# Matmul and transfer durations of a list schedule set to recorded ones

## The chip, the cores and the metric

The kernel runs on one core of one Trainium2 chip. A core has a matrix engine (TensorE, PE in the profile, with its weight loads as PEld), VectorE (DVE), ScalarE (ACT), GpSimd (POOL) and SyncE (SP), which here issues all DMA transfers between the chip's memory and the core's SBUF. TensorE writes its results to PSUM, which has eight banks of 512 words per partition. The metric is the time of one execution in microseconds on the device; lower is better.

## The reference

One layer of a decoder for 512 tokens of width 1024, in float32. A conditioning vector gives shift, scale and gate of two sub-layers (1024 x 6144 weights, `w_ada`). The mixer has two branches, joined by gates and an output projection; then comes an MLP with a squared ReLU.

```python
mod = c_act @ w_ada[l] + b_ada[l]
shift1, scale1, gate1, shift2, scale2, gate2 = [...]
h = rms_norm(x, g_pre_mix[l]) * (1.0 + scale1) + shift1
y = token_mixer(h, ...)
x = x + gate1 * rms_norm(y, g_post_mix[l])
h = rms_norm(x, g_pre_mlp[l]) * (1.0 + scale2) + shift2
y = jnp.square(jax.nn.relu(h @ w_mlp_in[l])) @ w_mlp_out[l]
x = x + gate2 * rms_norm(y, g_post_mlp[l])

# token_mixer
z = h @ w_in                               # 1024 x 4800
u = ua * jax.nn.sigmoid(ub)
u = causal_depthwise_conv(u, conv_w, conv_b)         # 31 taps
y_a = jax.nn.silu(layer_norm(u, ...)) @ w_conv_out
o = mla_attention(q_nope, q_rope, k_nope, k_rope, v) # 8 heads, causal
y_b = o @ w_attn_out
return (g_a * y_a + g_b * y_b) @ w_out
```

## The kernel before

**Arithmetic.** Most products are done on pairs: an operand is split into a high part (rounded to the engine's fp32r type by an ACT copy) and a low part (the difference, by a DVE subtraction), and a product is three matmuls, high x high, high x low, low x high (`mm3`). So each weight tile goes through a DMA load into the float arena (`f_arena`), an ACT cast and a DVE subtraction into the rounded arena (`r_arena`), and only then to TensorE (`wunit`, `W`).

**Stages, in program order.** The opening loads x, the parts of `w_ada` for the first modulation and the first columns of `w_in`, and multiplies them as they come. Then come the rest of `w_in` (gated-linear-unit columns, latents), attention head by head, the 31-tap convolution on DVE spread out between them (`pump`), `w_attn_out`, the two gates, the convolution branch's normalisation, `w_conv_out`, and `w_out`. The other parts of `w_ada` are accumulated on DVE (`ada_units`, one 1 MB load and two 128x1024 multiply-adds per step) at places set by `take`; parts 2 to 4 lie around the gates, `w_conv_out` and the beginning of `w_out`. After the norm between the sub-layers comes the MLP in four chunks; its second product uses Strassen's scheme with seven block products per chunk. The two arenas take 22400 and 28000 words per partition.

**The order of the work.** No instruction is issued when the program names it. `Planner.record` notes each one as an `Op` with its dependencies and a cost from `Planner.cost`: `o.cost`, the time for which it holds its engine, and `o.post`, the delay until its result can be used. `Planner.plan` then simulates the five engines:

- a first pass adds up TensorE's costs in program order; each TensorE op's sum is its deadline (`o.dead`), and the deadline of every other op is worked back from the ops that use it, with `o.cost`, `o.post` and, for a transfer, its bytes over 180 per ns;
- then, at each moment, every free engine takes from its heap of ready ops the one with the smallest key: on TensorE the program rank (`o.rank`, less a boost in a few places), on DVE, ACT, POOL and SP the deadline less `o.hurry`;
- a transfer holds SP for `o.cost`, starts 1100 ns after its issue or when the one modelled DMA path is free, takes its bytes over a rate, and lands 910 ns later.

`Planner.issue` (L383) emits the ops in that order, so each engine's instruction order is fixed by the plan, and on the chip each engine waits for semaphores where the plan's times don't hold.

**The places of buffers.** `Arena.alloc` and `Banks.alloc` give each buffer its place in SBUF or PSUM. A first emission has no times; after each plan, `Planner.lives` gives for every buffer the time from which it's wanted and the time at which it's let go, and the next emission places the buffers by these (`past`). A load's wanted time is at the earliest its deadline less `LEAD` (15000 ns). `emit` is repeated up to `PASSES` (8) times, and the plan with the smallest `plan.length` (the latest modelled end) is issued, its places replayed. So a duration in `cost` acts in three ways: on the order, on the places, and on which of the plans is taken.

All instructions that a plan issues have the profile's line L388, where they are emitted.

Of the kernel before, what the change touches and what calls it, by code (L numbers as in the profile page):

```python
# [53 lines left out]
class Arena:  # L54
# [11 lines left out]
    def __init__(self, tensor, words, past=None, replay=None):  # L66
        self.t = tensor
        self.n = words // self.G
        self.freed = [0.0] * self.n
        self.owner = [None] * self.n  # L70
        self.gone = []
        self.places = []
        self.past, self.replay = past, replay
        self.clock = 0.0
# [86 lines left out]


class Op:
    __slots__ = ("i", "eng", "fn", "a", "k", "cost", "post", "deps", "succ", "dead", "t0", "t1", "ndep", "ready", "dma", "rank", "hurry", "bufs", "raw")


class Planner:
# [6 lines left out]
    def __init__(self, nc, spaces):  # L174
        self.spaces = spaces
        self.real = dict(pe=nc.tensor, act=nc.scalar, dve=nc.vector, pool=nc.gpsimd, sp=nc.sync)
        self.ops = []
        self.last_w = {}
        self.reads = {}
        self.boost = 0  # L180
        self.hurry = 0.0
        self.after = None

    class Engine:
        def __init__(self, plan, name):
            self.plan, self.name = plan, name
# [30 lines left out]
    def cost(self, eng, fn, outs, ins, k):  # L217

        n = max(self.free_size(o) for o in (ins if fn == "reduce_sum" else outs))
        if fn == "dma_start":  # L220
            return 475.0, 2000.0
        psum = any(r.tensor.name.startswith("psum") for r in ins + outs)
        if eng == "pe":
            if fn == "transpose":
                return 0.85 * n + 1, 190.0
            if ins[0].dtype == F32:
                return max(53.5, n / 2.4 + 2) * 4, 190.0
            return max(64.0, n / 2.4 + 2.5), 190.0
        scalars = sum(isinstance(v, bass.AP) and self.free_size(v) == 1 for v in ins) if n > 1 else 0
        if eng == "act":  # L230
            t = 0.833 * n + (51 if psum else 93) + 93 * scalars
            if fn == "activation" and any(isinstance(v, bass.AP) for v in outs[1:]):
                t += 93
            return t, 150.0
        if eng == "dve":
            if fn in ("tensor_copy", "tensor_scalar"):
                return (1.04 if psum else 0.52) * n + 68 + 61 * scalars, 150.0
            if fn == "scalar_tensor_tensor":
                return 1.04 * n + 130, 150.0
            return 1.04 * n + 70, 150.0  # L240
        if fn == "memset":
            return 36.0, 100.0
        return (460.0 if ALU.pow in self.args else 160.0) + 1.0 * n, 150.0

    def record(self, eng, fn, a, k):
        self.args = a
        aps = [v for v in a if isinstance(v, bass.AP)]
        names = dict(k)
        outs, ins = [], []
        if "out" in names:  # L250
            outs.append(names.pop("out"))
        else:
            outs.append(aps.pop(0))
        if fn == "tensor_tensor_reduce":
            outs.append(aps.pop())
        if isinstance(names.get("accum_out"), bass.AP):
            outs.append(names.pop("accum_out"))
        ins = aps + [v for v in names.values() if isinstance(v, bass.AP)]
        o = Op()
        o.i, o.eng, o.fn, o.a, o.k = len(self.ops), eng, fn, a, k  # L260
        o.succ, o.dma, o.rank, o.hurry = [], None, len(self.ops) - self.boost, self.hurry
        o.cost, o.post = self.cost(eng, fn, outs, ins, k)
        if fn == "dma_start":
            b = 4
            for _, c in outs[0].ap:
                b *= c
            o.dma = b
        deps = set()
        rd = [self.region(r) for r in ins]
        wr = [self.region(w) for w in outs]  # L270
        o.bufs = set()
        for nm, units in rd + wr:
            for sp in self.spaces:
                if nm.startswith(sp):
                    o.bufs.add((sp, self.spaces[sp].owner[units[0]]))
        for nm, units in rd:
            lw, rs = self.last_w.setdefault(nm, {}), self.reads.setdefault(nm, {})
            for u in units:
                if u in lw:
                    deps.add(lw[u])  # L280
        o.raw = set(deps)
        for nm, units in wr:
            lw, rs = self.last_w.setdefault(nm, {}), self.reads.setdefault(nm, {})
            for u in units:
                if u in lw:
                    deps.add(lw[u])
                if u in rs:
                    deps.update(rs[u])
        for nm, units in rd:
            rs = self.reads[nm]  # L290
            for u in units:
                rs.setdefault(u, []).append(o.i)
        for nm, units in wr:
            lw, rs = self.last_w[nm], self.reads[nm]
            for u in units:
                lw[u] = o.i
                rs.pop(u, None)
        deps.discard(o.i)
        if self.after is not None:
            deps.add(self.after)  # L300
        o.deps = deps
        for d in deps:
            self.ops[d].succ.append(o.i)
        self.ops.append(o)

    def plan(self):
        ops = self.ops
        pe_t = 0.0
        big = sum(o.cost for o in ops if o.eng == "pe") + TAIL
        for o in ops:  # L310
            o.dead = big
            if o.eng == "pe":
                pe_t += o.cost
                o.dead = pe_t
        for o in reversed(ops):
            lat = o.post + (o.dma / 180.0 if o.dma else 0.0)
            for s in o.succ:
                q = ops[s]
                o.dead = min(o.dead, q.dead - q.cost - lat)
        heaps = {e: [] for e in self.NAMES}  # L320
        free = {e: 0.0 for e in self.NAMES}
        dma_free = 0.0
        future = []

        def key(o):
            return (o.rank, o.i) if o.eng == "pe" else (o.dead - o.hurry, o.i)

        for o in ops:
            o.ndep, o.ready = len(o.deps), 0.0
            if not o.ndep:  # L330
                heapq.heappush(future, (0.0, o.i))
        order = []
        now = 0.0
        while len(order) < len(ops):
            while future and future[0][0] <= now:
                o = ops[heapq.heappop(future)[1]]
                heapq.heappush(heaps[o.eng], (key(o), o.i))
            for e in self.NAMES:
                if free[e] <= now and heaps[e]:
                    o = ops[heapq.heappop(heaps[e])[1]]  # L340
                    o.t0 = now
                    free[e] = now + o.cost
                    if o.dma:
                        st = max(now + 1100.0, dma_free)
                        dma_free = st + o.dma / 360.0
                        o.t1 = dma_free + 910.0
                    else:
                        o.t1 = free[e] + o.post
                    order.append(o)
                    for s in o.succ:  # L350
                        q = ops[s]
                        q.ndep -= 1
                        q.ready = max(q.ready, o.t1 if (q.eng != o.eng or o.dma) else free[e] if e == "pe" else max(free[e], o.t1 - 30))
                        if not q.ndep:
                            heapq.heappush(future, (q.ready, q.i))
            nxt = [free[e] for e in self.NAMES if free[e] > now and heaps[e]]
            if future:
                nxt.append(future[0][0])
            if not nxt:
                break  # L360
            now = max(now, min(nxt)) if min(nxt) > now else now
        assert len(order) == len(ops)
        self.length = max(o.t1 for o in ops)
        return order
# [1270 lines left out]
```

## Time and profile before

| | |
|---|---|
| time, median of 3 runs | 832.8 us (831.78 to 833.91) |
| time of the profiled execution | 832.68 us |
| its span, first to last instruction | 830.9 us |
| mean granted TensorE clock | 0.994 |
| ACT busy in the span | 422.4 us (51%) |
| DMA, all queues | 117.28 MB, mean 141 GB/s |

The page splits the span into 40 slices of 20.8 us. A digit is a slice's busy share in tenths; PEclk is the granted clock and DMA the busy share of the 16 DMA engines.

```profile
PE   6989999999999999999999989999999999999995
DVE  4979989999999999998999589298529993975696
PEclk9999999999999999999999999999999999999998
DMA  9998423201464140062799362065014831660302
```

A group of instructions is shown with its engine, its operation, output and inputs with their shapes, its count, its busy time, the mean duration of one, and the engine's idle time just ahead with what ended it. Instructions overlap in an engine's pipeline, so a busy time is less than count times mean. A row of busy times by stretch has the stretch in us from the span's start, its length, and then for PE, PEld, DVE, ACT and POOL the busy time with the count, then the granted clock, the DMA share and GB/s. A timeline row has start, duration, engine, line, operation and count.

### The profile page before, as it was taken

Reading aid. Unit: us, or ns where it says so; the run is one execution under the profiler, and the core shown is the slowest. Engines: PE = TensorE matmul, PEld = TensorE weight load, DVE = VectorE, ACT = ScalarE, POOL = GpSimd, SP = SyncE. Lnnn points to the kernel's source line nnn. Section 1 sums busy time; section 2 is a strip of 40 time slices with the busy share of each in tenths; the row PEclk is TensorE's granted clock in tenths of the full one; section 3 lists DMA queues with packets and bytes.
Section 4 is the critical chain, followed back from the end, with each engine's and each line's share of the span. In section 5 each row is a group of like instructions: output and inputs, shape, how many; then the busy total and the mean of one; then the engine's idle time right before and its main releaser. Section 6 shows DMA issues by size and latency. Waiting matters only on the chain.

```text
span 830.9 us, 10647 instructions
## 1 busy us (share of the span) xinstructions
PE 805.1 (97%) x3940; PEld 672.5 (81%) x3940; DVE 686.6 (83%) x1012; ACT 422.4 (51%) x712; POOL 26.4 (3%) x84
## 2 busy tenths in 40 slices
PE   6989999999999999999999989999999999999995
PEld 3867888889987888888877879888888888888884
DVE  4979989999999999998999589298529993975696
ACT  5364273275884356218424387375346354554642
POOL 2001020000000000000000020000000000000001
PEclk9999999999999999999999999999999999999998
DMA  9998423201464140062799362065014831660302
GB/s 309 321 301 261 153 70 95 71 27 44 135 176 116 40 126 26 26 229 76 277 341 374 118 205 79 27 195 160 0 51 149 277 131 52 193 212 1 102 0 103
DMA packets 86824, 117.28 MB, mean 141 GB/s; under 512 B 7275, under 2 KB 60628, under 8 KB 86771
## 3 DMA queue, kind: packets, MB, share of 16 engines
q1 hardware_dynamic: 86770, 116.59, 43.6%
q8 instruction: 31, 0.51, 0.2%
q14 instruction: 23, 0.18, 0.1%
HBM read 108.18 MB, written 8.39 MB: 140 GB/s over the span
## 4 chain that ended last, share of the span: by engine, by line
PE 87%; DVE 6%; DMA 4%; ACT 2%; issue 1%; POOL 0%; POOLq 0%; DVEq 0%; ACTq 0%; SPq 0%
PE psum L388 87%; DVE f_arena L388 4%; DMA f_arena<-in_w_in_dram 2%; DVE r_arena L388 1%; ACT f_arena L388 1%; DMA f_arena<-in_w_out_dram 1%; ACT r_arena L388 1%; POOL stats L388 0%; DMA f_arena<-in_x_dram 0%; DMA f_arena<-in_w_ada_dram 0%; ACT stats L388 0%; POOLq L1630 0%; DVE mod L388 0%; DVEq L1630 0%; DVE cols L388 0%
## 5 line engine op out<-in xcount | busy, mean ns | idle before, releaser
L388 PE MATMUL psum<-r_arena 128*128 128x512 f32 (+3 forms) x3592 | 765.7, 373 | 8.5 <-ACT r_arena L388 3.6
L388 PEld LDWEIGHTS psum<-r_arena 128*128 128x128 f32 x3592 | 631.3, 189 | 126.8 <-ACT r_arena L388 4.9
L388 DVE TENSOR_TENSOR r_arena<-f_arena,r_arena 128x1024 fp32r<-128x1024 f32 (+4 forms) x232 | 248.1, 1093 | 97.2 <-PE psum L388 56.2
L388 ACT CAST r_arena<-f_arena 128x1024 fp32r<-128x1024 f32 (+4 forms) x222 | 209.3, 967 | 189.7 <-PE psum L388 123.5
L388 DVE SCALAR_TENSOR_TENSOR f_arena<-f_arena,cw 128x512 f32<-128x512 f32 x240 | 164.5, 748 | 0.0
L388 ACT ACTIVATE f_arena<-psum 128x512 f32<-128x512 f32 x64 | 38.1, 598 | 131.4 <-PE psum L388 124.6
L388 DVE TENSOR_TENSOR f_arena<-f_arena 128x1024 f32<-128x1024 f32 (+3 forms) x78 | 77.3, 1006 | 5.5 <-ACT f_arena L388 3.6
L388 ACT ACTIVATE f_arena<-f_arena 128x512 f32<-128x512 f32 (+3 forms) x100 | 58.5, 606 | 13.5 <-DVE f_arena L388 12.6
L388 DVE SCALAR_TENSOR_TENSOR f_arena<-f_arena,cT 128x256 f32<-128x256 f32 (+2 forms) x84 | 55.3, 705 | 0.2
L388 PE MATMUL psum<-ident,f_arena 128*128 128x128 f32 (+1 forms) x240 | 34.4, 283 | 7.5 <-DVE f_arena L388 7.5
L388 PEld LDWEIGHTS psum<-ident,f_arena 128*128 128x128 f32 (+1 forms) x240 | 28.9, 146 | 12.8 <-DVE f_arena L388 8.2
L388 DVE TENSOR_TENSOR f_arena<-psum,f_arena 128x512 f32<-128x512 f32 x52 | 35.4, 687 | 4.4 <-PE psum L388 4.3
L388 ACT CAST r_arena<-psum 128x512 fp32r<-128x512 f32 (+2 forms) x57 | 30.3, 567 | 16.6 <-PE psum L388 16.4
L388 DVE TENSOR_TENSOR r_arena<-psum,r_arena 128x512 fp32r<-128x512 f32 (+2 forms) x57 | 35.7, 658 | 2.5 <-ACT r_arena L388 1.9
L388 POOL TENSOR_TENSOR stats<-stats,nhalf 128x1 f32<-128x1 f32 x24 | 16.8, 708 | 485.4 <-ACT stats L388 485.4
L388 ACT COPY f_arena<-psum 128x512 f32<-128x512 f32 (+4 forms) x42 | 19.9, 501 | 22.1 <-PE psum L388 21.9
L388 ACT ACTIVATE r_arena<-f_arena 128x512 fp32r<-128x512 f32 (+3 forms) x20 | 13.0, 648 | 18.7 <-DVE f_arena L388 16.2
L388 DVE CUSTOM_DVE_ANT_0 f_arena<-psum,mask 128x128 f32<-128x128 f32 (+3 forms) x32 | 15.2, 487 | 2.6 <-PE psum L388 2.5
L388 DVE SCALAR_TENSOR_TENSOR f_arena<-f_arena 128x512 f32<-128x512 f32 (+1 forms) x18 | 13.4, 747 | 0.3
L388 DVE SCALAR_TENSOR_TENSOR f_arena<-f_arena,psum 128x512 f32<-128x512 f32 x16 | 11.0, 685 | 3.1 <-PE psum L388 2.6
L388 DVE TENSOR_SCALAR f_arena<-f_arena,stats 128x1024 f32<-128x1024 f32 x8 | 6.0, 752 | 8.4 <-POOL stats L388 8.4
L388 DVE SCALAR_TENSOR_TENSOR f_arena<-psum,stats,f_arena 128x512 f32<-128x512 f32 x8 | 5.6, 748 | 8.5 <-POOL stats L388 8.3
(94 smaller groups left out, 188.0 us busy)
## 6 DMA issues: line engine op xcount, KB each, us to landing
f_arena<-in_w_ada_dram SPq DMA_DIRECT2D x16, 1024.0 KB, 8.2
f_arena<-in_w_mlp_in_dram SPq DMA_DIRECT2D x32, 512.0 KB, 4.3
f_arena<-in_w_mlp_out_dram SPq DMA_DIRECT2D x32, 512.0 KB, 5.2
f_arena<-in_w_in_dram SPq DMA_DIRECT2D x28, 512.0 KB, 4.7
f_arena<-in_x_dram SPq DMA_DIRECT2D x8, 512.0 KB, 8.0
f_arena<-in_w_ada_dram SPq DMA_DIRECT2D x16, 256.0 KB, 5.7
f_arena<-in_w_ada_dram SPq DMA_DIRECT2D x8, 512.0 KB, 6.4
h_spill<-r_arena SPq DMA_DIRECT2D x16, 256.0 KB, 4.1
```

What stands on the lines that cost most here:

```text
L388: getattr(self.real[o.eng], o.fn)(*o.a, **o.k)
```

## The change

Figures in `Planner.cost`, `Planner.record` and `Planner.plan` are changed, and an attribute `slack` is added.

- A matmul of n columns on rounded operands is planned at max(109, n/2.4 + 13.3) ns, where it was max(64, n/2.4 + 2.5). Transposes and float32 matmuls keep their costs.
- A transfer issued by SP holds it for 375 ns, where it was 475; one issued by POOL would hold it for 850.
- The modelled DMA path moves 320 bytes per ns, where it was 360; a transfer issued by POOL would count 1.7 times its bytes.
- `plan.slack`, 0.0 at the start, is added to a transfer's landing time.

```diff
-    __slots__ = (..., "bufs", "raw")
+    __slots__ = (..., "bufs", "raw", "slack")
...
         self.after = None
+        self.slack = 0.0
...
         if fn == "dma_start":
-            return 475.0, 2000.0
+            return 850.0 if eng == "pool" else 375.0, 2000.0
         psum = any(r.tensor.name.startswith("psum") for r in ins + outs)
         if eng == "pe":
             if fn == "transpose":
                 return 0.85 * n + 1, 190.0
             if ins[0].dtype == F32:
                 return max(53.5, n / 2.4 + 2) * 4, 190.0
-            return max(64.0, n / 2.4 + 2.5), 190.0
+            return max(109.0, n / 2.4 + 13.3), 190.0
...
         o.cost, o.post = self.cost(eng, fn, outs, ins, k)
+        o.slack = self.slack
         if fn == "dma_start":
             b = 4
             for _, c in outs[0].ap:
                 b *= c
-            o.dma = b
+            o.dma = b * 1.7 if eng == "pool" else b
...
                     if o.dma:
                         st = max(now + 1100.0, dma_free)
-                        dma_free = st + o.dma / 360.0
-                        o.t1 = dma_free + 910.0
+                        dma_free = st + o.dma / 320.0
+                        o.t1 = dma_free + 910.0 + o.slack
```

More of the change, by code (lines that the diff above doesn't have):

```diff
@@ L163 @@
 class Op:
-    __slots__ = ("i", "eng", "fn", "a", "k", "cost", "post", "deps", "succ", "dead", "t0", "t1", "ndep", "ready", "dma", "rank", "hurry", "bufs", "raw")
+    __slots__ = ("i", "eng", "fn", "a", "k", "cost", "post", "deps", "succ", "dead", "t0", "t1", "ndep", "ready", "dma", "rank", "hurry", "bufs", "raw", "slack")
 class Planner:
```

## The prediction

> **What bounds the kernel now.** I read the page first (span, engines, chain), then busy time by stage, then the stages that hold idle TensorE time. The page's span line, TensorE's line and the chain:
>
> ```profile
> span 830.9 us, 10647 instructions
> PE 805.1 (97%) x3940; PEld 672.5 (81%) x3940; DVE 686.6 (83%) x1012; ACT 422.4 (51%) x712; POOL 26.4 (3%) x84
> PE 87%; DVE 6%; DMA 4%; ACT 2%; issue 1%; POOL 0%; POOLq 0%; DVEq 0%; ACTq 0%; SPq 0%
> ```
>
> TensorE is busy for 805.1 of 830.9 us. The change adds and removes no instruction; it can only alter the order on each engine and the places of buffers. So it works on the other 25.8 us and on the granted clock, and on nothing else. Busy time by stage (start:end, length, each engine's busy us with its count, granted clock, DMA share, GB/s):
>
> ```profile
> 0.00:7.25 7.25, 0.00 (x0) 0.00 (x1) 0.75 (x1) 4.36 (x8) 3.35 (x45) 1.00 0.75 276
> 7.25:70.00 62.75, 59.34 (x272) 43.55 (x272) 49.79 (x119) 33.31 (x48) 3.54 (x12) 1.00 1.00 308
> 70.00:420.00 350.00, 349.65 (x1823) 298.59 (x1824) 331.92 (x572) 180.71 (x365) 10.06 (x17) 1.00 0.36 112
> 420.00:460.00 40.00, 37.22 (x159) 29.75 (x158) 36.87 (x42) 12.21 (x14) 0.00 (x0) 0.96 1.02 370
> 460.00:490.70 30.70, 28.02 (x135) 22.77 (x134) 19.46 (x26) 17.03 (x44) 4.69 (x7) 1.00 0.37 128
> 490.70:505.00 14.30, 14.30 (x118) 14.09 (x119) 13.48 (x22) 13.37 (x28) 2.16 (x2) 1.00 0.63 213
> 505.00:818.90 313.90, 313.90 (x1429) 261.86 (x1428) 227.12 (x225) 159.10 (x203) 0.73 (x1) 1.00 0.33 106
> 818.90:830.90 12.00, 2.69 (x12) 1.88 (x11) 7.25 (x11) 2.33 (x7) 1.83 (x3) 0.73 0.37 139
> ```
>
> Length less busy gives TensorE's idle time by stage: 7.25, 3.41, 0.35, 2.78, 2.68, 0, 0, 9.31; sum 25.78. The first 7.25 us (x lands and is normalised) and most of the last 9.31 (statistics, scaling and store after the last matmul) are dependencies that no order removes. The MLP, from 490.7 to 818.9, has no gap: nothing can be won there, only lost. What an order can win lies in four places: 3.41 us in the opening, where the DMA share is 1.00; 2.78 us around 437; 2.68 us in the norm between mixer and MLP; and part of the tail.
>
> The gap around 437, in TensorE's timeline, then in that of the other engines, then in stretches of 2 us:
>
> ```profile
> 434.22 0.63 PE L388 MATMUL psum<-r_arena,onesr 128*128 128x512 f32 x2
> 437.29 1.20 PE L388 MATMUL psum<-r_arena 128*128 128x512 f32 x4 [2.44 <-ACT r_arena L388]
> 438.76 6.39 PE L388 MATMUL psum<-r_arena 128*128 128x512 f32 x20 [0.27 <-DVE r_arena L388]
> ```
>
> ```profile
> 429.76 1.28 DVE L388 SCALAR_TENSOR_TENSOR f_arena<-f_arena,cT 128x1024 f32<-128x1024 f32 x1
> ...
> 431.07 0.37 SPq L388 DMA_DIRECT2D f_arena<-in_w_out_dram  x1
> ...
> 436.19 1.57 ACT L388 CAST r_arena<-f_arena 128x1024 fp32r<-128x1024 f32 x2 [1.89 <-DMA f_arena<-in_w_out_dram]
> ```
>
> ```profile
> 438.00:440.00 2.00, 1.73 (x6) 1.10 (x5) 2.00 (x3) 0.00 (x0) 0.00 (x0) 0.68 1.04 346
> 440.00:442.00 2.00, 2.00 (x6) 1.52 (x6) 2.00 (x2) 1.05 (x1) 0.00 (x0) 0.50 1.03 374
> 442.00:444.00 2.00, 2.00 (x10) 1.68 (x9) 2.00 (x3) 0.00 (x0) 0.00 (x0) 0.96 1.06 395
> ```
>
> The reader is to see a chain: a w_ada accumulation (DVE, operand cT) ends at 431.04, SP issues a w_out load at 431.07, ACT's cast waits for w_out, TensorE waits 2.44 us for the cast, then 0.27 for the low half. Then the granted clock falls: (1 - 0.68), (1 - 0.50), (1 - 0.96) times 2 us each is 1.72 us lost. The place costs 2.71 + 1.72 = 4.43 us.
>
> On the clock: here an idle stretch of 2.44 us was enough for half clock. [...]
>
> **The change part by part.** First the matmul durations. TensorE's forms over the whole run, then the same view from 505 to 818.9 us, where nothing waits:
>
> ```profile
> L388 PE MATMUL psum<-r_arena 128*128 128x512 f32 x2962 | 690.5, 392 | 6.1 <-ACT r_arena L388 3.6 <-DVE r_arena L388 2.4
> L388 PE MATMUL psum<-r_arena 128*128 128x256 f32 x418 | 54.7, 284 | 2.4 <-ACT f_arena L388 2.4
> L388 PE MATMUL psum<-r_arena 128*128 128x384 f32 x58 | 12.6, 337 | 0.0
> L388 PE MATMUL psum<-r_arena 128*128 128x192 f32 x96 | 10.9, 274 | 0.0
> L388 PE MATMUL psum<-r_arena 128*128 128x128 f32 x58 | 8.1, 263 | 0.0
> ```
>
> ```profile
> L388 PE MATMUL psum<-r_arena 128*128 128x512 f32 x1333 | 302.5, 389 | 0.0
> L388 PE MATMUL psum<-r_arena 128*128 128x256 f32 x92 | 11.2, 283 | 0.0
> ```
>
> Undisturbed, 302.5/1333 = 226.9 ns at 512 columns and 11.2/92 = 121.7 ns at 256. The old formula gives 215.8 and 109.2, the new one 226.6 and 120.0: for the two forms that hold most of the time the new figures are right. Old to new, the planner's TensorE time grows by 10.8 ns x (2962 + 418 + 58) + 26.5 ns x 96 + 45 ns x 58 = 37.1 + 2.5 + 2.6 = 42 us, some 5%. Not one matmul runs faster or slower for it.
>
> [...]
>
> What does it move? TensorE's own heap goes by rank, so its order changes only where readiness does. VectorE, ScalarE and SyncE are served by `dead - hurry`, and a plan believes an engine full or free by these durations. In 70 to 420 us, with the old figures, the recorded 349.65 us of TensorE shrink to 349.65 x 215.8/226.9 = 332.5 (an estimate: all taken as 512 wide), against 331.92 of DVE, which is 100% full; with the new ones DVE is 95% full. DVE's own figures, which stay, are right: VectorE's timeline has
>
> ```profile
> 379.30 3.07 DVE L388 TENSOR_TENSOR f_arena<-f_arena,psum 128x512 f32<-128x512 f32 x5
> 382.29 0.68 DVE L388 SCALAR_TENSOR_TENSOR f_arena<-f_arena 128x512 f32<-128x512 f32 x1
> ```
>
> five in a row start (382.29 - 379.30)/5 = 0.598 us apart, and the formula says 0.602. One more stretch of the busy times:
>
> ```profile
> 360.00:380.00 20.00, 20.00 (x101) 16.82 (x100) 16.23 (x38) 6.79 (x17) 1.40 (x1) 1.00 0.63 211
> ```
>
> A plan that believes DVE full serves convolution taps and splits by deadline and leaves the w_ada accumulations last, which is where the chip runs them, against w_out. Yet on the chip DVE was idle for 350 - 331.92 = 18.1 us of that stage, and for 20 - 16.23 = 3.77 us in 360 to 380 alone: room for two accumulations of 1.28 us if their loads have landed, which is what the wait of 2.44 needs. The new plan sees that room. So I take the gap at 437 as closed: **-4.43 us**. Bounds: 0 if the room is spent elsewhere, -4.43 if it goes whole. What is late next is the following split or load; the nearest rows are the opening's short waits, in the list of waits:
>
> ```profile
> PE psum L388 <- DVE r_arena L388: 2.4, 4, 0.9
> ```
>
> 0.6 us each. I charge two, **+1.2 us** (bounds 0 and the whole row, 2.4).
>
> Second, the transfers. The issue falls from 475 to 375 ns, and the w_out issue row above took 0.37 us. The rate falls from 360 to 320 bytes per ns; the trace has 308 GB/s in the opening and 370 from 420 to 460, both at a full DMA share. The opening becomes truer, the stage with the gap less true: its 370 x 40 = 14.8 MB take 40 us, the old plan said 41.1, the new one says 46.3. In the opening DMA stays full whatever the order; I take **0**, with -1.7 to +1.7 for one 512 KB load (0.52 MB at 308 GB/s) put earlier or later in it.
>
> The norm (2.68 us) is a chain of statistics: **0**. In the tail
>
> ```profile
> 822.04 1.41 DVE L388 SCALAR_TENSOR_TENSOR f_arena<-f_arena,stats 128x512 f32<-128x512 f32 x2
> 823.37 0.69 DVE L388 TENSOR_TENSOR f_arena<-psum,f_arena 128x512 f32<-128x512 f32 x1
> ```
>
> the last product's sum stands behind two scalings; the other order would win up to 1.41 us. Nothing says that it flips: **0**, bounds -1.41 and 0.
>
> Third, `slack` stays 0.0 and every transfer of the kernel is issued from `sp`, so the slack and the two POOL factors do nothing; no work is moved to POOL's queue, and on SP's the number of issues is the same. No wait is added by hand.
>
> Sum: -4.43 + 1.2 = -3.2 us. The profiled execution took 832.68 us (its span and 1.8 us around it), 0.1 below the median of 832.8, so **829.5 us**.
>
> **The rivals.**
> - *The gaps only move* (or the plan comes out as it was). For it: four fifths of the idle time (7.25 + 3.41 + 2.68 + some 8 of the tail) are dependencies or a full DMA, DVE is busy 36.87 of 40 us from 420 to 460, and its idle 18 us lie in many small pieces. Against: 3.77 of them lie together, just ahead. Time: 832.7, give or take 2.5. The 0.3% that a measurement of this kernel can tell from no change is 2.5 us.
> - *The slower bandwidth spoils the burst.* The new plan has the burst's end 6.3 us late, so buffers are given and loads ranked for arrivals that aren't the chip's, and one 1 MB w_ada load goes out ahead of the w_out load that ACT waits for. Price: 1.05 MB at 370 GB/s is 2.8 us more wait, and a second loss of clock like the first, 1.72: +4.5, so 837.2. It decides once that w_out load is issued later than now, that is less than 434.22 - 431.07 = 3.15 us before TensorE's last earlier work starts. For it: the burst is the one stage where the new figure is further off; against: the deadline of a load doesn't use this rate.
>
> **How the numbers follow.** Forecast 0.45, gaps move 0.31, spoiled burst 0.24; these are the chances of faster, within 0.3%, and slower. Low end: -4.43 - 1.7 - 1.41 = -7.5, so 825. High end: the spoiled burst with most of its error, 838. The forecast's own range is 825 to 830.2.
>
> **What would show it.** Right: the TensorE gap near 437 under 1 us and the clock there at 1.00; w_ada accumulations denser before 412; DVE idle less than 18.1 us in 70 to 420; the MLP still without gaps. Wrong: the w_out cast still waiting for DMA, a gap over 0.5 us inside the MLP, or more than 3.4 us of idle TensorE in the opening.

## The result, and the profile after

| | before | after |
|---|---|---|
| time, median | 832.99 us (831.78 to 833.91, 4 runs) | 840.02 us (839.24 to 840.43, 4 runs) |
| ratio to before, 95% interval | | 1.0082 [1.0061, 1.0104] |
| time of the profiled execution | 832.68 us | 840.18 us |
| its span | 830.9 us | 838.4 us |

The change makes the kernel slower by 0.8%, 7 us. The forecast was 829.5 us with a range of 825 to 838; the time lies 10.5 us above the one and 2 us above the other. Among the runs below, one execution (of the loads spread) showed a granted clock of 0.85 and took 903.9 us; it isn't counted in that median.

The page of the kernel after, its span line, its TensorE line and three rows of slices (a slice is 21 us):

```profile
span 838.4 us, 10645 instructions
...
PE 810.2 (97%) x3940; PEld 675.1 (81%) x3940; DVE 685.5 (82%) x1012; ACT 421.9 (50%) x712; POOL 34.1 (4%) x84
...
PE   6979999989999999999999999999999999999995
...
PEclk9989999999999999999999999999999999999998
DMA  9796703320254232353899033056004831560302
```

The 8 that TensorE's row had in its 24th slice (the norm) is gone. New are a 7 in the third slice (42 to 63 us), with the clock at 8, an 8 in the ninth (168 to 189), and in the second slice a DMA share of 7 where it was 9. POOL's busy time has gone from 26.4 to 34.1 us though its work is the same. Busy time by stage (stretch, length, then PE, PEld, DVE, ACT, POOL with their counts, granted clock, DMA share, GB/s), cut as for the kernel before, the last two stretches moved by the 7.5 us that the span has grown:

```profile
0.00:7.25 7.25, 0.26 (x1) 0.27 (x2) 0.75 (x1) 4.36 (x8) 3.65 (x46) 1.00 0.71 251
7.25:70.00 62.75, 57.62 (x249) 42.04 (x249) 49.31 (x116) 29.90 (x43) 2.43 (x10) 0.95 0.97 303
70.00:420.00 350.00, 344.02 (x1785) 291.79 (x1784) 333.82 (x572) 178.82 (x364) 19.22 (x17) 1.00 0.38 120
420.00:460.00 40.00, 40.00 (x178) 33.10 (x178) 35.25 (x42) 16.65 (x20) 0.00 (x0) 1.00 1.01 352
460.00:490.70 30.70, 30.41 (x144) 24.80 (x143) 11.25 (x17) 9.23 (x26) 2.31 (x4) 1.00 0.15 53
490.70:505.00 14.30, 14.04 (x97) 12.65 (x96) 12.79 (x20) 14.08 (x31) 2.46 (x4) 1.00 0.54 181
505.00:826.40 321.40, 321.16 (x1485) 268.50 (x1485) 235.10 (x236) 166.56 (x216) 2.02 (x2) 1.00 0.33 107
826.40:838.40 12.00, 2.72 (x12) 1.91 (x11) 7.25 (x11) 2.33 (x7) 2.02 (x3) 0.73 0.37 139
```

Length less busy is idle TensorE time. To it I add the time lost to the clock: (1 - granted clock) times TensorE's busy time, summed over stretches of 1 us. A cell of this table is idle + lost clock in us; the rows of all kernels below are made the same way.

| stretch, us | before | after | difference |
|---|---|---|---|
| 0 to 20 | 7.2 + 0 | 7.0 + 0 | -0.2 |
| 20 to 80, opening | 3.4 + 0 | 5.1 + 3.2 | +4.9 |
| 80 to 420, attention and on | 0.3 + 0 | 6.0 + 1.7 | +7.3 |
| 420 to 460, the gap at 437 | 2.8 + 1.7 | 0 + 0 | -4.4 |
| 460 to 515, norm | 2.7 + 0 | 0.8 + 0 | -1.9 |
| last 12 | 9.3 + 0 | 9.3 + 0 | 0 |
| whole | 25.8 + 1.7 | 28.2 + 4.9 | +5.7 |

So 5.7 of the 7.5 us have a place; 1.8 us lie in TensorE's busy time with no stretch that stands out, and stay unplaced. What the change was forecast to win came, and more: 6.3 us from 420 to 515. It was given back nearly twice over, 12.2 us, at two places for which the forecast had 1.2 us together.

**The opening.** SyncE's timeline, kernel after (start, duration, operation, count):

```profile
14.68 2.75 SPq L390 DMA_DIRECT2D f_arena<-in_w_ada_dram  x4
17.47 3.19 SPq L390 DMA_DIRECT2D f_arena<-in_w_in_dram  x4
20.70 0.34 SPq L390 DMA_DIRECT2D rows<-in_g_pre_mlp_dram  x1
22.17 0.29 SPq L390 DMA_DIRECT2D rows<-in_conv_b_dram  x1
23.66 0.27 SPq L390 DMA_DIRECT2D rows<-in_conv_norm_g_dram  x1
25.16 0.27 SPq L390 DMA_DIRECT2D rows<-in_conv_norm_b_dram  x1
25.84 0.24 SPq L390 DMA_DIRECT2D rows<-in_q_norm_g_dram  x1
...
27.47 0.23 SPq L390 DMA_DIRECT2D f_arena<-in_conv_w_dram  x1
27.81 0.40 SPq L390 DMA_DIRECT2D f_arena<-in_w_ada_dram  x1
```

and the same queue before:

```profile
21.52 0.30 SPq L388 DMA_DIRECT2D rows<-in_g_pre_mlp_dram  x1
23.03 0.29 SPq L388 DMA_DIRECT2D rows<-in_conv_b_dram  x1
24.58 0.40 SPq L388 DMA_DIRECT2D f_arena<-in_w_ada_dram  x1
```

Eight small loads (1 to 4 KB, and 124 KB of taps; two rows are left out) now stand in a row where two stood. Each takes SP 0.23 to 0.34 us, yet they start 1.5 us apart at first, and the last four, up to 27.47, some 0.5 us ((27.47 - 25.84)/3). What holds them, in the list of SP's waits from 14 to 48 us (total in us, times, longest):

```profile
SPq L390 <- PE psum L390: 3.9, 2, 2.4
SPq L390 <- DVE f_arena L390: 3.8, 5, 1.4
SPq L390 <- DMA f_arena<-in_w_ada_dram: 3.5, 3, 1.2
SPq L390 <- DMA f_arena<-in_w_in_dram: 1.3, 4, 0.4
```

The small loads wait, as the last two lines say, for loads to land with which they share no buffer. The trace has eight semaphores on which transfers land, and SP's 269 transfers take them in turn. For 98 transfers the trace of before tells when the one eight places ahead landed: none of them starts before that, the closest 0.02 us after it; of the 98 for which it tells when the one seven places ahead landed, 17 start before. So I read it thus: in this program SP starts no transfer until the one eight places ahead has landed. (The first two lines, 7.7 us, are large loads that wait for buffers which TensorE and DVE free, most of it behind the row: SP stands at two `w_ada` loads from 29.79 to 35.08 us. That is a rival reading of the late opening.) The first four small loads have 512 KB loads eight places ahead of them, and they start 1.5 us apart: 0.52 MB at the 357 GB/s that the trace has from 20 to 25 us is 1.47 us. So the row takes 27.81 - 20.70 = 7.1 us, where the new plan counts 8 x 0.375 = 3.0; meanwhile the large loads in flight run out, and no new one is started. Two stretches of 5 us, kernel after:

```profile
25.00:30.00 5.00, 5.00 (x23) 4.09 (x23) 4.97 (x15) 2.48 (x3) 0.00 (x0) 1.00 0.42 136
...
45.00:50.00 5.00, 4.08 (x13) 2.77 (x13) 4.96 (x14) 1.86 (x2) 0.12 (x1) 0.68 1.00 286
```

The DMA share falls to 0.42 from 25 to 30 us. Twenty microseconds later TensorE has used up what had been loaded, as its timeline shows (in brackets the idle time and what ended it), and its clock falls to 0.68:

```profile
45.62 0.61 PE L390 MATMUL psum<-ones,f_arena 128*128 128x1 f32 x4 [3.15 <-DVE f_arena L390]
...
50.43 0.60 PE L390 MATMUL psum<-ones,f_arena 128*128 128x1 f32 x4 [0.73 <-DVE f_arena L390]
...
52.26 2.23 PE L390 MATMUL psum<-r_arena 128*128 128x512 f32 x7 [1.23 <-ACT r_arena L390]
```

**The start of attention.** Timelines of DVE, POOL, ACT and TensorE, kernel after:

```profile
99.94 12.69 DVE L390 SCALAR_TENSOR_TENSOR f_arena<-f_arena,cw 128x512 f32<-128x512 f32 x19
...
103.91 10.29 POOL L390 TENSOR_TENSOR stats<-stats,nhalf 128x1 f32<-128x1 f32 x1 [25.95 <-ACT stats L390]
...
114.23 0.62 ACT L390 ACTIVATE f_arena<-f_arena,stats 128x384 f32<-128x384 f32 x1 [9.47 <-POOL stats L390]
...
122.06 0.76 DVE L390 TENSOR_TENSOR f_arena<-f_arena,rp 128x256 f32<-128x256 f32 x2 [5.65 <-ACT f_arena L390]
...
139.63 29.09 PE L390 MATMUL psum<-r_arena 128*128 128x512 f32 x144 [1.56 <-DVE f_arena L390]
...
172.06 0.65 PE L390 MATMUL psum<-ident,f_arena 128*128 128x128 f32 x4 [3.34 <-DVE f_arena L390]
```

Read it downwards. POOL raises one number per partition to a power; in the kernel after, the others of its kind take 0.55 to 1.29 us, this one 10.29, while DVE runs 19 convolution taps back to back (one per 12.69/19 = 0.67 us). ACT, whose next instruction reads that result, stands 9.47 us behind it, then DVE 5.65 us behind ACT, and TensorE, which has a store of finished operands, comes to the end of it at 139.63 and at 172.06. After the second wait the clock falls again:

```profile
174.00:176.00 2.00, 2.00 (x12) 2.00 (x11) 1.74 (x3) 1.91 (x4) 0.00 (x0) 0.50 0.01 4
```

### The profile page after: what moved, and what is told of

Same layout as the page of the kernel before. It is cut to its first block, busy times and chain, and to the rows that moved or that the text cites. A ratio compares the mean times of both kernels' runs of the same rounds, so it can differ in the third digit from the quotient of the medians.

```text
span 838.4 us, 10645 instructions
## 1 busy us (share of the span) xinstructions
PE 810.2 (97%) x3940; PEld 675.1 (81%) x3940; DVE 685.5 (82%) x1012; ACT 421.9 (50%) x712; POOL 34.1 (4%) x84
## 4 chain that ended last, share of the span: by engine, by line
PE 77%; DVE 12%; ACT 5%; POOL 2%; DMA 2%; issue 1%; DVEq 0%; POOLq 0%; SPq 0%; ACTq 0%
PE psum L390 77%; DVE f_arena L390 8%; DVE r_arena L390 3%; ACT f_arena L390 3%; ACT r_arena L390 2%; POOL stats L390 2%; DMA f_arena<-in_w_in_dram 1%; ACT stats L390 0%; DMA f_arena<-in_x_dram 0%; POOL lns L390 0%; DVE lns L390 0%; POOLq L1632 0%; DVEq L1632 0%; DVE mod L390 0%; SPq L390 0%
## 5 line engine op out<-in xcount | busy, mean ns | idle before, releaser
L390 PE MATMUL psum<-r_arena 128*128 128x512 f32 (+2 forms) x3592 | 767.5, 374 | 3.5 <-DVE f_arena L390 1.8
L390 DVE SCALAR_TENSOR_TENSOR f_arena<-f_arena,cw 128x512 f32<-128x512 f32 x240 | 167.4, 754 | 0.0
L390 ACT ACTIVATE f_arena<-f_arena 128x512 f32<-128x512 f32 (+4 forms) x100 | 58.7, 603 | 20.4 <-DVE f_arena L390 19.2
L390 PE MATMUL psum<-ident,f_arena 128*128 128x128 f32 (+1 forms) x240 | 36.1, 289 | 10.9 <-DVE f_arena L390 10.8
L390 POOL TENSOR_TENSOR stats<-stats,nhalf 128x1 f32<-128x1 f32 x24 | 26.3, 1097 | 482.5 <-ACT stats L390 482.4
L390 ACT CAST r_arena<-psum 128x512 fp32r<-128x512 f32 (+2 forms) x57 | 30.4, 563 | 17.3 <-PE psum L390 16.2
L390 ACT ACTIVATE r_arena<-f_arena 128x512 fp32r<-128x512 f32 (+3 forms) x20 | 13.0, 650 | 19.0 <-DVE f_arena L390 16.2
L390 ACT ACTIVATE f_arena<-f_arena,lnh 128x512 f32<-128x512 f32 x16 | 12.5, 812 | 3.5 <-DVE f_arena L390 3.5
```

The lines of the kernel that those rows point to most:

```text
L390: getattr(self.real[o.eng], o.fn)(*o.a, **o.k)
```

## The experiments

Two theories came out of this reading. *Opening*: the shorter issue time puts the small loads in a row ahead of `w_ada`, and SP's wait for the transfer eight places ahead turns that into idle DMA (a share of 0.42 from 25 to 30 us). *POOL*: the new order puts one POOL operation beside a run of taps that starves it. The rivals: each figure has a price of its own and they add up; it is the places of the buffers and not the order; the loads of the opening wait for buffers that come free late, whatever the small loads do; or any new order is a throw of dice. All ratios are to runs of the kernel before on the same chip, medians of runs (their number in brackets).

**The three figures one by one, and two by two.** The kernel before with one line of the diff, or two:

```diff
# e1: matmuls
-            return max(64.0, n / 2.4 + 2.5), 190.0
+            return max(109.0, n / 2.4 + 13.3), 190.0
# e7: rate
-                        dma_free = st + o.dma / 360.0
+                        dma_free = st + o.dma / 320.0
# e8: issue
-            return 475.0, 2000.0
+            return 375.0, 2000.0
# e9: matmuls and rate; e10: matmuls and issue
```

Matmuls alone:

> The kernel before with the new matmul figures alone (109 ns, n/2.4 + 13.3); issue 475 and rate 360 stay. Theory M: the loss comes from the matmul figures, since a plan that gives TensorE 42 us more sees DVE and ACT with room everywhere and packs them without regard to what the chip makes of it: 838 to 841 us, with a TensorE gap of 3 us or more at 100 to 180 us. Theory D: the loss comes from the transfers' figures, in the opening above all: 830 to 834 us, the opening's gaps under 3.5 us. Theory C: any new figure throws the order, and which one is a matter of luck: anything from 828 to 842, with gaps at places that neither kernel has.

Rate alone:

> The kernel before with the new rate alone (320 instead of 360). The matmul figures alone gave 832.8, so the opening's loss (late w_ada loads, TensorE waiting at 45 to 52 us) is put down to the transfers' figures. Theory R (the rate): the planner believes the opening's loads late, gives buffers that TensorE frees late, and the loads wait for them: 836 to 841, the opening's idle TensorE time 5 us or more. Theory I (the issue time does it): 830.5 to 834, the opening like that of before. Theory C (luck of a new order, no figure's own doing): anywhere from 829 to 842, the loss at a place that the other kernels don't have.

Issue time alone:

> The kernel before with the new issue time alone (375 instead of 475). Theory I: SyncE comes free sooner in the plan, takes the small row loads eight in a row because they need no buffer, and the opening loses 4 to 6 us: 836 to 840. Theory R: 830.5 to 834, the row loads spread as before. Theory C: anything from 829 to 842.

Matmuls and rate:

> Matmul figures and rate together, issue time as before. Theory R: the opening's loss, without or with the long operation on POOL: 836 to 841. Theory I: 831 to 834. If the figures add up, time follows from the single ones: 832.8 plus what the rate alone adds to 832.7; if they don't (theory C), it differs from that by 2.5 us or more.

Matmuls and issue time:

> Matmul figures and issue time together, rate as before. Theory I: 836 to 841 with eight row loads in a row. Theory R: 831 to 834. If the figures add up, 832.8 plus what the issue time alone adds; theory C: off that sum by 2.5 us or more.

Measured (the last four columns are idle + lost clock, as above; from 420 to 460 us all five have none):

| kernel | median us (n) | ratio [95%] | 20 to 80 | 80 to 420 | 460 to 515 | small loads in the first row |
|---|---|---|---|---|---|---|
| e1 matmuls | 832.8 (8) | 1.0012 [0.9992, 1.0032] | 2.7 + 1.7 | 3.5 + 0 | 0.9 + 0 | 2 |
| e7 rate | 830.0 (6) | 0.9977 [0.9963, 0.9992] | 2.9 + 0 | 0.5 + 0 | 3.4 + 1.6 | 5 |
| e8 issue | 835.2 (8) | 1.0037 [1.0020, 1.0053] | 6.8 + 1.6 | 0.3 + 0 | 2.7 + 1.7 | 8 |
| e9 matmuls, rate | 834.4 (8) | 1.0009 [0.9993, 1.0026] | 4.9 + 1.7 | 4.5 + 1.7 | 1.6 + 0 | 5 |
| e10 matmuls, issue | 842.1 (2) | 1.0110 [1.0076, 1.0144] | 9.4 + 4.5 | 4.2 + 1.7 | 0.8 + 0 | 8 |
| after | 840.0 (4) | 1.0082 [1.0061, 1.0104] | 5.1 + 3.2 | 6.0 + 1.7 | 0.8 + 0 | 8 |

The stretches are those of the profiled execution, which in e1 and e8 lies 1.5 and 2.1 us below the median.

What follows. The prices don't add: against the medians of before beside them, matmuls and issue time alone bring some +0.2 and +2.4 us, together +9.4. But the stretches sort themselves. The row of eight small loads, and an opening that loses over 8 us, come with the issue time of 375 ns and only with it (e9, with five in a row, comes nearest: 6.6). Here more than 0.5 us is lost between 80 and 420 us only with the new matmul durations, and the norm's gap shrinks only with them. The gap at 437 is in none of them, not even where the matmul durations are the old ones: in e7, for one, whose stretches of 420 to 460 and 460 to 490 us are

```profile
420.00:460.00 40.00, 40.00 (x187) 33.28 (x185) 39.73 (x49) 14.34 (x21) 0.00 (x0) 1.00 0.99 356
460.00:490.00 30.00, 26.59 (x126) 21.66 (x125) 21.23 (x29) 20.69 (x51) 5.57 (x7) 0.96 0.62 215
```

**POOL given its turn.** The kernel after, in which DVE, just after the fifth of POOL's powers has been issued, copies its result to a scrap of SBUF, so that DVE waits for POOL once:

```diff
+            if o.eng == "pool" and o.a[-1] is ALU.pow:
+                pows += 1
+                if pows == 5:
+                    self.real["dve"].tensor_copy(self.scratch, o.a[0])
```

> The changed kernel, same order and places, with one 128x1 copy on DVE that reads the result of the fifth reciprocal root on POOL, the one that took 10.29 us from 103.91 while DVE ran 19 convolution taps in a row; so DVE pauses there until POOL is through. Theory P (POOL can't get in while DVE runs tap after tap, ACT's queue stands behind it for 9.47 us, DVE then for 5.65, and the gaps of 1.56 at 139.6 and 3.34 at 172.1 with the clock at 0.91 are its end): the operation under 1.5 us, ACT's wait under 1.5, the gaps at 139 and 172 gone or under 1 us together, 840.0 - 4.9 - 1.7 = 833.4, that is 832.5 to 835.5. Rival: the gaps come from DVE's own order (taps ahead of the sums that free PSUM and of the rotary products): the operation short, the gaps within 1 us of what they were, 839 to 841.

Measured: 833.4 us (8), ratio 1.0010 [0.9991, 1.0029], against 1.0082 without it: some 6 us for one 128x1 copy. The timelines of DVE and POOL in that kernel:

```profile
100.49 4.06 DVE L391 SCALAR_TENSOR_TENSOR f_arena<-f_arena,cw 128x512 f32<-128x512 f32 x6
...
104.44 0.57 POOL L391 TENSOR_TENSOR stats<-stats,nhalf 128x1 f32<-128x1 f32 x1 [25.95 <-ACT stats L391]
...
105.05 0.15 DVE L395 COPY scratch<-stats 128x1 f32<-128x1 f32 x1 [0.49 <-POOL stats L391]
105.12 8.69 DVE L391 SCALAR_TENSOR_TENSOR f_arena<-f_arena,cw 128x512 f32<-128x512 f32 x13
```

DVE waits 0.49 us, POOL is done in 0.57, and the same 19 taps go on (6 + 13). From 80 to 420 us 1.3 us are lost in place of 7.7; the opening keeps its loss (5.5 + 3.0). The POOL theory is shown for the kernel after: nothing else was edited. It isn't the whole of what the new matmul durations cost there: in e10 five such powers take 4.10 us together, and it loses 4.2 + 1.7 us from 80 to 420 all the same; what holds e10 up stays open.

**The small loads spread.** The kernel after, in which the six loads of rows are held back at issue and let go one by one, after every second further load; and this together with the copy above:

```diff
+            if o.fn == "dma_start" and o.k["out"].tensor.name.startswith("rows1"):
+                held.append(o)
+                continue
...
+            if o.fn == "dma_start" and held:
+                loads += 1
+                if loads % 2 == 0:
+                    h = held.pop(0)
+                    getattr(self.real[h.eng], h.fn)(*h.a, **h.k)
```

> The changed kernel, same order otherwise, with the six small row loads (4 KB and less, on SP from 20.70 to 26.41 us) held back and issued one after every second further load. Each load waits for the one eight places ahead of it to end, so eight small ones in a row leave nothing in flight (DMA share 0.42 from 25 to 30 us). Theory L (that run of small loads makes the opening late): the share from 25 to 30 over 0.8, the w_ada load of 27.81 issued two to four us sooner, the gap of 3.15 us at 45.6 under 1, the clock there at 1.00: 840.0 - 3 to 6, so 834 to 837. Rival: the loads wait for buffers that TensorE frees later than before (its first products end at 23.5 where they ended at 21.6), and the small loads only fill the time: 838.5 to 841.

> Both edits. If theories P and L hold and the two places are apart: the sum of the two savings, 827 to 831, faster than the kernel before, since the gap at 437 and most of the norm's are gone in the changed kernel. If either rival holds: the other's saving alone, 833 to 837. If what is won early is given back later (a wait that stands behind the removed ones): 835 or more though both places are clean.

Measured: 836.9 us (7), ratio 1.0063 [1.0042, 1.0084], and both together 830.5 us (10), 0.9974 [0.9960, 0.9989]. The first is a half miss. The DMA share from 25 to 30 us rose from 0.42 to 0.88, but it was 0.39 in the next 5 us, and 5.0 + 3.1 us were still lost from 20 to 80. The edit holds back the six rows alone; the load of positions and that of the taps (`conv_w`, 124 KB) now come first, at 19.41 and 20.82. The `w_ada` load that goes out at 32.18 stands eight places behind the taps' load, and the list of SP's waits from 14 to 48 us has for it

```profile
SPq L394 <- DMA f_arena<-in_conv_w_dram: 2.4, 1, 2.4
```

So a small load held the queue up again, another one and 5 us later: that speaks for the wait eight places ahead, but what the opening is worth without it this edit, which moves loads by count and not by need, doesn't show. Its time is 3.1 us better than the kernel after's by the medians, and its stretches don't show where from. With both edits the sum came out as forecast, but not by the two savings that were to make it: the opening still loses 4.9 + 1.5 us.

**The order, or the places.** The whole change, but with the search for places at one issue time and the final order planned at the other:

```diff
+    ISSUE = 475.0
...
+            return Planner.ISSUE, 2000.0
...
-    if plan is not best:
+    Planner.ISSUE = 375.0
+    if True:
         plan = emit({}, {n: a.places for n, a in best.spaces.items()})
```

Above is e11, with places from 475 and the order from 375; e12 has the two numbers exchanged.

> The changed kernel, with the buffers' places searched at an issue time of 475 (those of matmul and rate together, 834.4) and only the last ordering made at 375. SyncE's order in the opening comes out with eight small loads in a row, as in the changed kernel. Theory O (the order that 375 gives is what costs, wherever the buffers lie): 838 to 842, 7 us or more of idle TensorE time and lost clock from 20 to 60 us. Theory B (the places): 833 to 835.5, as matmul and rate together.

> The changed kernel, with the places searched at 375 and only the last ordering made at 475. SyncE's order comes out with five small loads in a row and the other three further on. Theory O: 833 to 836, 5 us or less of idle time and lost clock from 20 to 60 us. Theory B: 838.5 to 841, as the changed kernel.

Measured: the order of 375 gives 839.2 us (2), ratio 1.0093 [1.0072, 1.0113]; the order of 475 gives 832.2 us (8), 1.0007 [0.9992, 1.0023]. From 20 to 80 us they lose 4.8 + 3.2 and 2.1 + 0; from 80 to 420, 4.1 + 1.6 and 4.6 + 1.7. So it's the order in the opening that the issue time spoils; the places, which went the other way, hardly matter. The late buffers don't explain it either: SP's waits for buffers from 14 to 48 us, 7.7 us in the kernel after, are 7.5 us in the kernel before and 9.0 in e12, whose openings lose 3.4 and 2.1. e12 also shows that the two losses are separate: it keeps the second one (its POOL operation takes 8.92 us) without the first.

**The plan told of the eight transfers.** The kernel after with all its figures, and a plan in which a transfer holds SP until the one eight places ahead has landed; and the same edit in the kernel before, with the old figures (360 in the rate's line):

```diff
+        lands = []
...
-                        st = max(now + 1100.0, dma_free)
+                        go = max(now, lands[-8]) if len(lands) >= 8 else now
+                        free[e] = go + o.cost
+                        st = max(go + 1100.0, dma_free)
                         dma_free = st + o.dma / 320.0
                         o.t1 = dma_free + 910.0 + o.slack
+                        lands.append(o.t1)
```

> The changed kernel, with one thing added to the plan: a transfer can't be issued before the one eight places ahead of it has landed, as the waits of SyncE's queue on the chip are; figures as changed. In the plan a small load is then no cheaper for SyncE than a large one, and the six row loads come after the last w_ada and w_in loads of the opening. Theory I in this form (the plan's SyncE is too free, so at 375 it fills the queue with small loads): idle time and lost clock from 20 to 60 us under 4 us where the changed kernel has 8.3; 833 to 836, less if POOL's long operation is gone as well (down to 829). Rival (w_ada and w_in loads wait for buffers that TensorE and DVE free late, whatever the small loads do): the opening loses 6 us or more, 837 to 841.

> The kernel before, with its own figures (475 ns, 360 bytes per ns, the old matmul durations), and the eight outstanding transfers put into the plan as in the lanes run with the changed figures (827.1). Theory 'the lanes decide, the figures count for little once they are there': no TensorE gap over 1 us from 20 to 80 us (the kernel before has 1.61 and 1.81 there), the gap at 437 gone as in every other variant, the norm's gap (2.68) kept as in the runs with the old matmul durations: 832.7 - 3.4 - 4.4 = 825 to 829.5. Theory 'true matmul durations are worth something of their own': the norm's gap stays and short gaps appear in 70 to 420 us, where DVE looks too full to the plan: 829.5 to 832. Rival 'the run with the lanes was one lucky order of many': gaps over 1 us in the opening, or 832.5 to 840.

Measured: with the changed figures 827.1 us (826.36 to 830.02, 8 runs), ratio 0.9951 [0.9936, 0.9966]; with the old ones 829.1 us (827.56 to 830.75, 10 runs), 0.9960 [0.9944, 0.9976]. Both are faster than before, by 0.5% and 0.4%, and 1.3% faster than the kernel after (0.9951/1.0082 = 0.987). SP's timeline in the first:

```profile
20.59 5.03 SPq L394 DMA_DIRECT2D f_arena<-in_w_ada_dram  x4
25.71 4.13 SPq L394 DMA_DIRECT2D f_arena<-in_w_in_dram  x4
...
42.44 0.40 SPq L394 DMA_DIRECT2D rows<-in_g_pre_mlp_dram  x1
...
46.78 0.23 SPq L394 DMA_DIRECT2D f_arena<-in_conv_w_dram  x1
```

and one stretch of it, where the kernel after had a DMA share of 0.42:

```profile
25.00:30.00 5.00, 5.00 (x22) 4.11 (x23) 4.94 (x15) 2.39 (x3) 0.00 (x0) 1.00 1.09 354
```

All eight small loads now stand behind the large ones, at 42.44 to 47 us; DMA is full from 25 to 30 (1.09), and TensorE doesn't stop from 20 to 60. The row still empties the DMA queues, with a share of 0.39 from 45 to 50 us, but no gap of TensorE over 0.8 us follows. The whole run loses 20.1 + 0 us, the fewest of all kernels. With the old figures and the same wait in the plan it is 22.4 + 0, in the fastest of its ten runs. This bears the opening theory out from the other side: that wait, once planned for, takes the loss away at either issue time. The whole order changes with it, though, so that it works by the small loads alone isn't shown. (That the number is eight, and not seven or nine, wasn't tried.)

Does the truth of the figures count once the wait is in the plan? The intervals of the two overlap and the runs weren't made side by side, so 2.0 us in favour of the true figures is not settled. And "dice" isn't refuted altogether: from 80 to 420 us both lose less than 2 us (1.9 and 1.8), and the POOL loss is absent, though nothing in their plans knows of it. In e13 the powers even stand beside a run of taps:

```profile
105.67 5.39 DVE L394 SCALAR_TENSOR_TENSOR f_arena<-f_arena,cw 128x512 f32<-128x512 f32 x8
107.43 4.04 POOL L394 TENSOR_TENSOR stats<-stats,nhalf 128x1 f32<-128x1 f32 x6 [37.82 <-ACT stats L394]
```

Six of them take 4.04 us, 0.67 each, which is one per tap. So a run of taps doesn't always keep POOL out; why it did so in the kernel after and not here stays open.

## Why the prediction was wrong

- **Matmul durations truer:** nothing in the runs speaks against it, and yet e1, which has this alone, is no faster, 1.0012. A true figure bought no time by itself.
- **Accumulations go earlier:** right, and to be seen in every kernel with the new matmul durations. Of the 32 multiply-adds of 128x1024 with `cT`, 14 start before 412 us where 8 did, and the last before the norm starts at 453.88 us before and at 435.41 after:

```profile
435.41 1.28 DVE L390 SCALAR_TENSOR_TENSOR f_arena<-f_arena,cT 128x1024 f32<-128x1024 f32 x1
```

  With the old matmul durations it starts at 453 to 460 us (before, e7, e8, e14), with the new ones at 424 to 440 (e1, e9 to e13 and after). DVE's idle time from 70 to 420 us is 350 - 333.82 = 16.2 us, under the 18.1 of before, as put.
- **The gap at 437 goes, -4.43:** the event came and the reason fell. It went in the kernel after and in all twelve variants, also where the accumulations stay late (e7, e8, e14). It belonged to the one order of the kernel before, and all ten other orders tried here lose it. That the 4.4 us came was luck, as far as the reason given goes.
- **The norm, 0:** wrong by 1.9 us in the kernel's favour. Here is where the earlier accumulations pay: 2.1 to 5.0 us are lost from 460 to 515 with the old matmul durations, 0.8 to 1.6 with the new ones. It was taken for a chain that no order shortens, without asking what DVE still did ahead of it.
- **Two short waits, +1.2:** the term that failed. It was sized at the opening's 0.6 us waits, without any loss of clock; the new waits are 3.15, 1.23 and 0.73 us in the opening and 1.56 and 3.34 at the start of attention, and the clock takes 4.9 us on top. In the sum for these two stretches, 12.2 us stand where 1.2 stood.
- **Opening, 0, within 1.7:** wrong, by 4.9 us. The step compared 375 ns with the 0.37 us of an issue row, found it truer, and concluded that DMA stays full; its share fell to 0.42. A row's duration isn't the time until the next row: SP's own starts, 1.5 us apart at small loads in the trace of before, were there to be read. The old 475 ns was further from the row and nearer to the chip.
- **Slack and POOL factors, 0:** nothing in the runs speaks against it. **Tail, 0:** right, 9.3 us in both.
- **The MLP without gaps:** right; its stretch has 0.24 us, at its start.
- **The rivals.** "Gaps only move" had the right idea and a wrong price: 6.3 us of gaps and lost clock went and 12.2 came. "The slower rate spoils the burst" named slower, but by luck: from 420 to 460 nothing is lost, and the rate alone makes the kernel faster, 0.9977. More than 3.4 us of idle TensorE in the opening was named as a sign against the forecast; it is 5.1.

## What to carry to other kernels

A list schedule's figure isn't right because it matches an instruction's duration: it stands also for the constraints that the model leaves out, and correcting it alone uncovers them. So before correcting a duration, compare planned and real *start-to-start* times on each queue, and put the missing constraint in first; here five lines for the transfer eight places ahead brought what the true figures didn't. And when a change can only reorder, price the places that are quiet now as well as the gaps: here 350 quiet microseconds came to hold 7.3 us of new loss.

## What the runs showed of the hardware

- A 128x1 operation on POOL took 10.29 us beside back-to-back taps on DVE (8.92 in e12, with DVE busy all the while), and 0.57 when DVE paused for 0.49. In e13 six powers beside taps take 0.67 us each, the time of one tap (5.39/8). In the kernel after POOL was held not for one tap of 0.67 us but for a run of them (10.29/0.67 is 15), and no run here shows why.
- In the kernel after, a small load in SP's queue cost the landing of the load eight places ahead: 1.5 us behind loads of 0.52 MB, 0.5 to 0.7 behind smaller ones, against 0.23 to 0.34 us of its own. And with the loads spread, the 124 KB of taps made the load eight places behind wait 2.4 us.
- In the kernel after, the clock falls after a single idle stretch of 3.15 us (to 0.68 over 5 us) or 3.34 us (to 0.50), and not after 1.56 us. The length of a stretch doesn't settle it in these runs: at the norm, 2.43 us in the kernel before left the clock at 1.00 and 2.44 us in e8 brought it to 0.50, and in e1 it was 0.50 from 72 to 74 us after 1.13 us of idle TensorE between 68 and 70 us. 3.3 of the 7.5 us are lost clock; e13, with no idle stretch above 0.8 us between its first 8 us and its tail, lost none.
